# Routing from the un-normalised residual in a two-layer mixture-of-experts stage, with the norm's scale and bias applied after the gather

## The chip, the cores and the metric

The kernel runs on one core of one Trainium2 chip. The metric is device time in microseconds (us) of one execution, as a median over runs. Four blocks run one after the other in it: two layers of attention and mixture of experts (layers 0 and 1), then a recurrent block and a windowed-attention block. The change touches the first two.

## What is computed

From the reference, for each of the two layers (T = 256 tokens, D = 1024, 16 experts of 512 columns, two experts for each token, all fp32):

```python
mix = hybrid_mixer(x, ...)                                    # its last step: concatenate(...) @ w_o
x = layer_norm(ALPHA * x + mix, ln1_g[l], ln1_b[l])
ffn = grouped_moe(x, router_w, router_bias, w_gate[l], w_up[l], w_down[l])
x = layer_norm(ALPHA * x + ffn, ln2_g[l], ln2_b[l])

def grouped_moe(h, router_w, router_bias, w_gate, w_up, w_down):
    aff = sigmoid(xt @ router_w)
    biased = aff + router_bias
    # best group of four experts by its top two, then the top two experts of that group
    wts = aff of the two, divided by their sum
    act = silu(xt @ w_gate[e]) * (xt @ w_up[e]) * gates[e]
    out = sum over e of act @ w_down[e]
```

Only the tokens that chose an expert need its product. The normalised row is (x - mean) * rstd * g + b; mean and rstd belong to the token, g and b to the column.

## The kernel before

Activations stand as two tiles of 128 tokens by 1024 columns (`xn`) and, transposed, as a high and a low fp32r part (`xh`, `xl`). A product with a weight is three fp32r products: high by high, low by high, high by low.

**End of the mixer.** `down` multiplies by `w_o` into four PSUM banks `y[token tile][column half]`. Its last four row chunks run token tile by token tile, so `y[0][0]` is ready about three banks ahead of `y[1][1]`. `layer_norm` then adds the residual, takes the moments (BN_STATS, BN_AGGREGATE, a square root on ScalarE), applies mean, g, rstd and b on VectorE, and transposes the result on TensorE; `logits` multiplies the transposed rows by the split router weights `rwhl`, and `router` turns logits into choices: a sigmoid, then a chain of some thirty small VectorE instructions that ends in the slot numbers `rs` and the one-hot matrices `P`.

**The experts.** `slots(g)` gathers the tokens of four experts as a matrix product of `P` with the rows `xnh`, `xnl` into `xTe`, and turns `P` and the gates (`pgt`, `pgs`, tile `gs`). Eight pairs of experts follow: `gate_up(p)` (`pgg`, then `pgu`), the transpose `pat`, `down` (`pdn`) for the pair before, and `spread`, which adds a pair's output into the four banks `py`. Each of `pgg`, `pgu` and `pdn` is 32 matmuls and uses four chunks of weights.

**The weights.** A layer has 96 chunks of 1 MB (two DMAs of 512 KB each), numbered 0 to 95 in the order of their use: per pair four for `pgg`, four for `pgu`, and four for `pdn` of the pair before. All go through SyncE's queue, which issues in order: a DMA that waits for its buffer holds up all that follow. The first 23 chunks (`FILL`, one letter each) have buffers of their own: `r` the ring, digits places that come free when the mixer's pools close, `m` the tile `misc`, `p` an `xh`/`xl` pair of buffers, `x` the tile `xn` itself. From chunk 23 on only the ring and the numbered places are used again, 18 in all, each as soon as TensorE has read it. `chunks()` asks for the first 23 before the first matmul of the experts.

`py` starts as a matmul that clears the bank and a ScalarE copy of ALPHA times `xn`. After that `xn` is free, so its chunk can load.

In both kernels TensorE's order in the experts is that of the program; on the other engines a scheduler sets the order when the kernel is built, and each engine then works in that order.

## Time and profile before

| | |
|---|---|
| median of 3 runs (1371.28 to 1372.64) | 1371.29 us |
| the profiled execution | 1371.13 us |
| its span, first to last instruction | 1369.5 us |
| TensorE busy | 1306.6 us, 95% |
| VectorE busy | 763.1 us, 56% |
| ScalarE busy | 583.2 us, 43% |
| GpSimd busy | 81.0 us, 6% |
| moved by DMA | 342.93 MB |

The span leaves out about 1.6 us that lie around the instructions. A busy TensorE is not TensorE at its peak, since the ends of matmuls are modelled; the pace of the starts tells more. All places in time below are counted from the start of the span.

### The profile page before, as it was taken

How to read it: one execution, taken by the hardware profiler on the slowest of the kernel's cores; microseconds unless marked ns; L12 is line 12 of the kernel's file. 1: busy time of each engine (PE TensorE's matmuls, PEld its weight loads, DVE VectorE, ACT ScalarE, POOL GpSimd, SP SyncE). 2: the span in 40 equal slices, each digit the busy share in tenths (PEclk: the TensorE clock that was granted, in tenths of full speed). 3: DMA queues.
4: the chain of work that ended last, by engine and by line, in shares of the span. 5: the costliest groups of instructions: out<-in, count | busy, mean ns of one | idle time of the engine just before them, and what ended most of it. 6: DMA issues, size and time to landing. Idle time of an engine off the chain costs nothing.

```text
span 1369.5 us, 20419 instructions
## 1 busy us (share of the span) xinstructions
PE 1306.6 (95%) x7941; PEld 955.6 (70%) x7941; DVE 763.1 (56%) x1584; ACT 583.2 (43%) x1110; POOL 81.0 (6%) x90
## 2 busy tenths in 40 slices
PE   7899899999998998999998999999999999999997
PEld 6787443444487664434435888889998887899986
DVE  4775510111368562111115678879886678888845
ACT  5684410101256841101103524556665376566642
POOL 3000100000200010000002143000000010000000
PEclk9999999999999999999999999999999999999999
DMA  9566699999981767999998820466554365575500
GB/s 299 192 236 256 240 408 398 416 418 416 324 304 70 277 244 290 393 416 417 417 416 290 287 96 29 157 214 214 185 202 136 126 216 171 181 234 185 199 18 31
DMA packets 153448, 342.93 MB, mean 250 GB/s; under 512 B 13282, under 2 KB 84840, under 8 KB 153345
## 3 DMA queue, kind: packets, MB, share of 16 engines
q1 hardware_dynamic: 149408, 330.14, 65.4%
q0 software_dynamic: 3616, 11.15, 2.4%
q8 instruction: 66, 1.08, 0.3%
q10 hardware_dynamic: 320, 0.26, 0.1%
q14 instruction: 38, 0.30, 0.1%
HBM read 340.44 MB, written 1.07 MB: 249 GB/s over the span
## 4 chain that ended last, share of the span: by engine, by line
PE 52%; DVE 3%; ACT 1%; issue 1%; DMA 0%; POOL 0%; DVEq 0%; ACTq 0%
PE pb L174 20%; PE y L174 12%; PE pv L174 3%; PE pdn L174 3%; PE pgg L174 3%; PE pgu L174 3%; PE pl L174 2%; PE ptk L174 2%; DVE xn L362 1%; PE py L174 1%; PE pkv L174 1%; PE po L174 1%; PE pt L228 1%; PE pg L174 1%; DVE wl L168 1%
## 5 line engine op out<-in xcount | busy, mean ns | idle before, releaser
L168 DVE TENSOR_TENSOR wl<-raw,wh 128x1024 fp32r<-128x1024 f32 (+1 forms) x208 | 248.3, 1199 | 86.2 <-ACT wh L167 84.3
L167 ACT ACTIVATE wh<-raw 128x1024 fp32r<-128x1024 f32 (+1 forms) x208 | 213.7, 1035 | 70.2 <-PE y L174 62.1
L1067 DVE SCALAR_TENSOR_TENSOR misc<-misc,gs,pgu 128x512 f32<-128x512 f32 x16 | 12.0, 747 | 226.8 <-PE pgu L174 149.8
L174 PE MATMUL pb<-xh,wh 128*128 128x256 f32 (+1 forms) x944 | 133.6, 281 | 0.5 <-ACT wh L167 0.5
L174 PE MATMUL pb<-xh,wl 128*128 128x256 f32 (+1 forms) x944 | 132.5, 281 | 1.6 <-DVE wl L168 1.6
L174 PE MATMUL pb<-xl,wh 128*128 128x256 f32 (+1 forms) x944 | 132.5, 280 | 0.0
L174 PEld LDWEIGHTS pb<-xh,wh 128*128 128x128 f32 (+1 forms) x944 | 120.3, 187 | 2.1 <-ACT wh L167 0.7
L174 PEld LDWEIGHTS pb<-xh,wl 128*128 128x128 f32 (+1 forms) x944 | 119.9, 187 | 2.2 <-DVE wl L168 2.0
L174 PEld LDWEIGHTS pb<-xl,wh 128*128 128x128 f32 (+1 forms) x944 | 119.9, 187 | 0.1
L174 PE MATMUL pgu<-raw,xTe 128*64 128x512 f32 x512 | 112.6, 592 | 0.0
L174 PE MATMUL pdn<-raw,misc 128*64 128x512 f32 x496 | 109.6, 592 | 0.0
L174 PE MATMUL pgg<-raw,xTe 128*64 128x512 f32 x448 | 103.0, 612 | 4.9 <-PEq L919 4.9
L167 ACT ACTIVATE xh<-pdn 128x512 fp32r<-128x512 f32 x32 | 19.1, 597 | 195.6 <-PE pdn L174 195.6
L174 PEld LDWEIGHTS pgu<-raw,xTe 128*64 128x64 f32 x512 | 37.7, 137 | 72.2 <-issue 68.7
L174 PEld LDWEIGHTS pdn<-raw,misc 128*64 128x64 f32 x496 | 36.4, 137 | 69.4 <-issue 64.4
L174 PEld LDWEIGHTS pgg<-raw,xTe 128*64 128x64 f32 x448 | 32.8, 140 | 65.1 <-issue 58.7
L168 DVE TENSOR_TENSOR xl<-pdn,xh 128x512 fp32r<-128x512 f32 x32 | 21.9, 686 | 100.4 <-ACT xh L167 88.5
L174 PE MATMUL y<-wl,gh 128*128 128x512 f32 x176 | 68.7, 390 | 0.0
L174 PE MATMUL y<-wh,gl 128*128 128x512 f32 x176 | 68.6, 390 | 0.0
L174 PE MATMUL y<-wh,gh 128*128 128x512 f32 x176 | 68.2, 389 | 0.0
L1066 ACT ACTIVATE misc<-pgg 128x512 f32<-128x512 f32 x16 | 9.6, 597 | 128.0 <-PE pgg L174 128.0
L174 PE MATMUL y<-wh,xl 128*128 128x512 f32 x128 | 51.4, 403 | 0.0
(357 smaller groups left out, 2267.1 us busy)
## 6 DMA issues: line engine op xcount, KB each, us to landing
raw<-in_w_up SPq DMA_DIRECT2D x128, 512.0 KB, 9.9
raw<-in_w_down SPq DMA_DIRECT2D x124, 512.0 KB, 9.9
raw<-in_w_gate SPq DMA_DIRECT2D x112, 512.0 KB, 10.0
raw<-in_ffn_w_in SPq DMA_DIRECT2D x44, 1024.0 KB, 6.0
raw<-in_ffn_w_out SPq DMA_DIRECT2D x22, 1024.0 KB, 5.1
raw<-in_hgrn_w_in SPq DMA_DIRECT2D x16, 1024.0 KB, 8.4
raw<-in_w_o SPq DMA_DIRECT2D x8, 1024.0 KB, 11.4
raw<-in_w_in SPq DMA_DIRECT2D x6, 1024.0 KB, 7.9
```

What stands on the lines that cost most here:

```text
L167: nc.scalar.activation(h, src, AF.Copy)
L168: (nc.gpsimd if pool else nc.vector).tensor_tensor(l, src, h.bitcast(F32), op=ALU.subtract)
L174: s.last = s.nc.tensor.matmul(out, lhsT, rhs, start=start, stop=stop, skip_group_check=True).ins
L228: return s.nc.tensor.transpose(out, in_, s.ident[:k, :k])
L362: prev.append(f(*a, **k).ins)
L1066: nc.scalar.activation(sg, ps[0], AF.Silu)
L1067: v.scalar_tensor_tensor(ac, sg, gs[:, p:p + 1], ps[1], op0=ALU.mult, op1=ALU.mult)
```

## The change

**Router.** The layer norm ahead of the experts is gone as a step of its own. TensorE transposes the raw residual r = ALPHA * x + mix. The router weights are multiplied by g and made free of their column mean on the chip (`router_weights`, once per layer, written behind the last weight split of `down`): with W the weights times g less their mean, r @ W times rstd plus a constant `rc` (from b) is the old logit. `aff` is formed by one VectorE instruction per token tile, with rstd as its scalar.

**Rows.** ScalarE writes (r - mean) * rstd, without g and b, into `xn` and `xnh`. `xnl` is made on GpSimd for token tile 0 and on VectorE for token tile 1. The gather's eviction applies g and b, which stand there as one scalar per partition (`gp`).

**First gather.** `slots(0)` uses eight PSUM banks at once, with the products of `xnl` of token tile 1 last, and all eight evictions behind them. Its `pgt`/`pgs` part moves between `pgg` and `pgu` of pair 0. Later calls use four banks at a time.

**Residual.** `py` is now formed by eight VectorE instructions (L1084: x * ALPHA * g in place; L1085: plus ALPHA * b into the bank) in place of four ScalarE copies. g and b as whole rows come by two DMAs on GpSimd's queue into an `xh`/`xl` pair (`gb1`).

**Loads.** The letters `p` and `x` are no longer in the first list; they are asked for behind `residual()`.

The diff, cut to its core:

```diff
-WARM_ROUTER = 8, 4
-WARM_LN = 12
+WARM_ROUTER = 14, 4
...
-    FILL = "rrrmr76rr54rr321rrp0ppx"
+    FILL = "rrrmr76rr54rr321rr0pppx"
...
+    def router_weights(s, li, t):
+
+
+        nc, v = s.nc, s.nc.vector
+        e3 = lambda o: t[:, o:o + 128].rearrange("p (k e) -> p k e", k=8)
+        rw, gw, bw, ones = e3(0), e3(128), e3(256), t[:, 384:512]
+        sums = t[:, 512:544].rearrange("p (a e) -> p a e", a=2)
+
+        with s.tc.issue_after(s.low):
+            v.memset(ones, 1.0)
+            for i, d in enumerate((gw, bw)):
+                v.tensor_tensor(d, rw, s.ln1(li, i)[:, :, None].to_broadcast([128, 8, 16]), op=ALU.mult)
+        p = s.pb("prw")
+        s.mm(p[:, :256], ones, t[:, 128:384], True, True)
+        v.tensor_reduce(sums, p[:, :256].rearrange("p (a k e) -> p a e k", a=2, k=8), axis=AX.X, op=ALU.add)
+        v.tensor_copy(s.rc, sums[:, 1])
+        v.tensor_scalar(sums[:, 0], sums[:, 0], 1.0 / D, None, op0=ALU.mult)
+        v.tensor_tensor(gw, gw, sums[:, 0, None, :].to_broadcast([128, 8, 16]), op=ALU.subtract)
         h = s.rwhl[:, :, 0:16]
-        keep(nc.scalar.activation(h, rw, AF.Copy))
-        keep(nc.vector.tensor_tensor(s.rwhl[:, :, 16:32], rw, h.bitcast(F32), op=ALU.subtract))
+        nc.scalar.activation(h, gw, AF.Copy)
+        v.tensor_tensor(s.rwhl[:, :, 16:32], gw, h.bitcast(F32), op=ALU.subtract)
...
-            gb = s.load_gb(mp, A["ln1_g"][li], A["ln1_b"][li], "kT")
+            rw = s.router_rows(mp.tile([128, 2048], F32, tag="kT", name="rw"))
...
-            s.lg = []
-            s.down(mh, ml, A["w_o"][li], 8, gb,
-                   after0=lambda: s.lg.append(s.logits(0)))
-
-    def down(s, mh, ml, w, nk, gb, col=None, out=None, hold=4, after0=None, pre=None, pool=()):
+            return s.down(mh, ml, A["w_o"][li], 8, None, pre=lambda: s.router_weights(li, rw))
...
+        def moments(b, q):
+            x = s.xn[:, b, q * 512:(q + 1) * 512]
+            seq(v.scalar_tensor_tensor, x, x, ALPHA, y[b][q], op0=ALU.mult, op1=ALU.add)
+            p = s.pb("pt")
+            for j in range(4):
+                s.tr(p[:, j * 128:(j + 1) * 128], x[:, j * 128:(j + 1) * 128])
+            pv = p.rearrange("p (a t) -> p a t", a=4)
+            h, l = (m.t[q][:, :, b * 128:(b + 1) * 128] for m in (xh, xl))
+            seq(act, h, pv, AF.Copy)
+            seq(v.bn_stats, st[b][:, q], x)
+            if q:
+                seq(v.bn_aggr, mv[b][:, 0:2], st[b])
+                seq(act, mv[b][:, 2:3], mv[b][:, 1:2], AF.Sqrt, bias=s.eps[:, 0:1])
+            return lambda: seq(v.tensor_tensor, l, pv, h.bitcast(F32), op=ALU.subtract)
...
+        def affinity(b):
+            lg = s.st.tile([32, 128], F32, tag="lg", name="lg", bufs=2)
+            seq(v.tensor_copy, lg, s.logits(b, xh, xl))
+            p = s.pb("psg")
+            with s.tc.issue_after(last_y):
+                s.mm(p[:, :16], lg, s.two, True, True)
+            return lambda: seq(v.scalar_tensor_tensor, aff[:, b], p[:, :16], mv[b][:, 3:4], s.rc, op0=ALU.mult,
+                               op1=ALU.add)
+
+        def normalized(b):
+            x = s.xn[:, b]
+            seq(act, x, x, AF.Identity, scale=mv[b][:, 3:4], bias=mv[b][:, 4:5])
+            seq(act, xnh[:, b].rearrange("p (c q) -> p c q", c=8), x.rearrange("p (q c) -> p c q", c=8), AF.Copy)
+
+        def low_rows(e, b, c):
+            n, h, l = (t[:, b].rearrange(f, c=8)[:, c] for t, f in ((s.xn, "p (q c) -> p c q"),
+                                                                 (xnh, "p (c q) -> p c q"), (xnl, "p (c q) -> p c q")))
+            return e.tensor_tensor(l, n, h.bitcast(F32), op=ALU.subtract)
...
+        with s.tc.high_priority():
+            low = [moments(0, 0), moments(0, 1)]
+            for f in low:
+                f()
+            scales(0)
+            low = moments(1, 0)
+            normalized(0)
+            seq(v.memset, pick, -BIG_NEG)
+            seq(v.memset, gs[:, 0], BIG_NEG)
+            low()
+            aff0 = affinity(0)
+            s.tc.keep_in_program_order(low_rows(nc.gpsimd, 0, slice(0, 8)))
+            low = moments(1, 1)
+            seq(act, sm[:, 0], s.eps, AF.Sigmoid)
+            gb = [x.rearrange("p a b -> p (a b)").bitcast(F32) for x in s.pair()]
+            for x, a in zip(gb, (s.A["ln1_g"][li], s.A["ln1_b"][li])):
+                s.tc.keep_in_program_order(nc.gpsimd.dma_start(x, bass.AP(tensor=a.tensor, offset=a.offset,
+                                                                          ap=[[0, 128], [1, D]])))
+            aff0()
+            low()
+            scales(1)
+            affinity(1)()
+            seq(act, aff, aff, AF.Sigmoid)
+            normalized(1)
...
-            py = [[s.pa("py") for _ in range(2)] for _ in range(2)]
-            for b in range(2):
-                for dh in range(2):
-
-                    s.mm(py[b][dh], s.negI, s.mgtb[:, None, :].to_broadcast([128, 4, 128]), True, False)
-                    keep(nc.scalar.activation(py[b][dh], s.xn[:, b, dh * 512:(dh + 1) * 512], AF.Copy, scale=ALPHA))
+            low_rows, gb1, ga, ov, rs, cnt = s.router(li, mp, y, xnh, xnl)
+            py = [[], []]
+
+            def residual():
+
+
+                for b in range(2):
+                    for dh in range(2):
+                        py[b].append(s.pa("py"))
+
+                        s.mm(py[b][dh], s.negI, s.mgtb[:, None, :].to_broadcast([128, 4, 128]), True, False)
+                for b in range(2):
+                    for dh in range(2):
+                        c = slice(dh * 512, (dh + 1) * 512)
+                        x = s.xn[:, b, c]
+                        v.scalar_tensor_tensor(x, x, ALPHA, gb1[0][:, c], op0=ALU.mult, op1=ALU.mult)
+                        v.scalar_tensor_tensor(py[b][dh], gb1[1][:, c], ALPHA, x, op0=ALU.mult, op1=ALU.add)
...
-            first = [i for i in range(n0) if i != m]
+            first = [i for i in range(n0) if i != m and s.FILL[i] not in "px"]
...
+                step = 4 if g else 8
+                for c0 in range(0, 8, step):
+
+                    ps = [(s.pa if i > 3 else s.pb)("pg") for i in range(step)]
+
+                    for bs in ((0, xnh), (0, xnl), (1, xnh)), ((1, xnl),):
+                        for c in range(c0, c0 + step):
+                            for b, x in bs:
+                                rhs = P[:, b].rearrange("p e s -> p (e s)")
+                                s.mm(ps[c - c0][:, :T], x[:, b, c * 128:(c + 1) * 128], rhs, b == 0 and x is xnh,
+                                     b == 1 and x is xnl)
+                    for c in range(c0, c0 + step):
+                        p, ga_, be = ps[c - c0][:, :T], s.gp[:, li, 0, c:c + 1], s.gp[:, li, 1, c:c + 1]
+                        if c % 2:
+                            nc.scalar.activation(xt[:, c], p, AF.Identity, scale=ga_, bias=be)
+                        else:
+                            i = v.tensor_scalar(xt[:, c], p, ga_, be, op0=ALU.mult, op1=ALU.add).ins
...
+            def gate_up(p, between=None):
                 x = xTe[p // 2][:, :, (p % 2) * 128:(p % 2) * 128 + 128]
                 ps = []
                 for nm in ("pgg", "pgu"):
+                    if ps and between:
+                        between()
...
+                P, i = onehot(0)
+                with s.tc.issue_after(i):
+                    for c in (0, 4):
+                        low_rows(v, 1, slice(c, c + 4))
+                i = slots(0, P)
                 for p in range(8):
-                    ac = gate_up(p)
+                    ac = gate_up(p, None if p else lambda: gates(0, P))
+                    if not p:
+                        with s.tc.issue_after(i):
+                            residual()
+
+                        for j in range(n0):
+                            load(j)
```

Three places in the built order show what moved. SyncE, layer 0, before: `raw` are the ring and the numbered places, `xh`/`xl` the letters `p`, `misc` the letter `m`, `xn` the letter `x`; the last row is the first chunk of a second use.

```order
L147 DMA raw_1759<-in_w_down 128x1024 x2
L147 DMA xh_1762<-in_w_down 128x1024
L147 DMA xl_1763<-in_w_down 128x1024
L147 DMA misc_1527<-in_w_gate 128x1024 x2
L147 DMA raw_1768<-in_w_down 128x1024 x2
L147 DMA xh_1771<-in_w_gate 128x1024
L147 DMA xl_1772<-in_w_gate 128x1024
L147 DMA xh_1775<-in_w_gate 128x1024
L147 DMA xl_1776<-in_w_gate 128x1024
L147 DMA xn_69<-in_w_gate 128x1024 x2
L147 DMA raw_1959<-in_w_gate 128x1024 x2
```

The same place in the changed kernel:

```order
L146 DMA raw_1743<-in_w_down 128x1024 x2
L146 DMA raw_1746<-in_w_down 128x1024 x2
L146 DMA misc_1450<-in_w_gate 128x1024 x2
L146 DMA xh_1816<-in_w_down 128x1024
L146 DMA xl_1817<-in_w_down 128x1024
L146 DMA xh_1820<-in_w_gate 128x1024
L146 DMA xl_1821<-in_w_gate 128x1024
L146 DMA xh_1824<-in_w_gate 128x1024
L146 DMA xl_1825<-in_w_gate 128x1024
L146 DMA xn_69<-in_w_gate 128x1024 x2
L146 DMA raw_1973<-in_w_gate 128x1024 x2
```

The order is nearly the same; the buffers are others. The third pair (`xh_1824`, `xl_1825`) is now the one that holds g and b for `residual()`, and `xn` is read by `residual()` too. The reuse of the ring stands behind both.

VectorE around pair 0 before, from the first gather's evictions to the copy of `pat`:

```order
L1037 COPY xTe<-pg 128x256 x4
L1050 COPY gs<-pgs 64x2 x2
L1023 TENSOR_TENSOR P<-c,R 128x256 x2
L1067 SCALAR_TENSOR_TENSOR misc<-misc,gs,pgu 128x512
L1074 COPY misc<-pat 128x512
```

And after:

```order
L1142 TENSOR_SCALAR xTe<-pg,gp 128x256 x4
L1084 SCALAR_TENSOR_TENSOR xn<-xn,xh 128x512 x4
L1161 COPY gs<-pgs 64x2 x2
L1119 TENSOR_TENSOR P<-c,R 128x256 x2
L1180 SCALAR_TENSOR_TENSOR misc<-misc,gs,pgu 128x512
L1085 SCALAR_TENSOR_TENSOR py<-xl,xn 128x512 x4
L1187 COPY misc<-pat 128x512
```

The first half of the residual (L1084) stands right behind the gather; the second half (L1085), the last reader of `xn` and of the pair's `xl`, stands behind the instruction that takes `pgu` of pair 0 (L1180).

TensorE at the end of `down` after the change; before, the same matmuls of `y` ran without `plt` between them, and `plt` came after two more transposes of token tile 1:

```order
L228 MATMUL pt<-c,xn 128x128 x4
L174 MATMUL plt<-xh,rwhl 32x128 x8
L174 MATMUL plt<-xl,rwhl 16x128 x8
L174 MATMUL y<-wl,xh 128x512
L174 MATMUL y<-wh,xl 128x512
L174 MATMUL y<-wh,xh 128x512
L174 MATMUL y<-wl,xh 128x512
L174 MATMUL y<-wh,xl 128x512
L174 MATMUL psg<-c,lg 128x16
L228 MATMUL pt<-c,xn 128x128 x4
```

The transposes and logits of token tile 0 now run inside the matmuls of `y`, and delay its last bank by their own time.

## Rows read from the trace of the kernel before

**Rows 1.** The page: what DMA moved in 40 equal slices of the span, GB/s.

```profile
GB/s 299 192 236 256 240 408 398 416 418 416 324 304 70 277 244 290 393 416 417 417 416 290 287 96 29 157 214 214 185 202 136 126 216 171 181 234 185 199 18 31
```

**Rows 2.** Timeline, TensorE, layer 0: start, length, line, operation, count [idle before].

```profile
162.47 5.37 PE L174 MATMUL pgg<-raw,xTe 128*64 128x512 f32 x24
...
169.39 7.04 PE L174 MATMUL pgu<-raw,xTe 128*64 128x512 f32 x32
177.34 0.66 PE L228 MATMUL pat<-c,misc 128*128 128x128 f32 x4 [0.92 <-DVE misc L1067]
...
348.16 7.04 PE L174 MATMUL pdn<-raw,misc 128*64 128x512 f32 x32
...
359.44 7.09 PE L174 MATMUL pdn<-raw,misc 128*64 128x512 f32 x32
```

**Rows 3.** Timeline, SyncE's DMA issues, layer 0.

```profile
150.51 1.36 SPq L147 DMA_DIRECT2D xn<-in_w_gate  x2
164.45 0.80 SPq L147 DMA_DIRECT2D raw<-in_w_gate  x2
...
326.10 18.93 SPq L147 DMA_DIRECT2D raw<-in_w_down  x16
```

**Rows 4.** Windows of layer 0: busy time by engine, granted clock, DMA share, GB/s.

```profile
158.00:160.00 2.00, 2.00 (x14) 2.00 (x14) 0.42 (x1) 0.76 (x2) 0.00 (x0) 0.73 0.05 12
...
170.00:180.00 10.00, 9.09 (x44) 3.06 (x42) 1.44 (x2) 1.52 (x2) 0.00 (x0) 1.00 1.00 375
...
210.00:220.00 10.00, 10.00 (x50) 3.39 (x48) 0.75 (x1) 0.60 (x1) 0.00 (x0) 1.00 0.99 351
...
300.00:310.00 10.00, 10.00 (x65) 6.84 (x62) 3.53 (x7) 2.35 (x5) 0.00 (x0) 1.00 1.02 416
```

**Rows 5.** DMA issues of 335 to 340 us: count, KB each, us to landing.

```profile
raw<-in_w_down SPq DMA_DIRECT2D x5, 512.0 KB, 9.9
```

**Rows 6.** The same of 343 to 346 us.

```profile
raw<-in_w_down SPq DMA_DIRECT2D x2, 512.0 KB, 12.6
...
gb<-in_ln_b POOLq DMA_DIRECT2D x1, 512.0 KB, 8.7
```

**Rows 7.** Timeline, VectorE, from the last residual add to the one-hot matrices.

```profile
138.28 0.69 DVE L362 SCALAR_TENSOR_TENSOR xn<-xn,y 128x512 f32<-128x512 f32 x1
...
140.83 2.20 DVE L362 SCALAR_TENSOR_TENSOR xn<-xn,mv,gb 128x512 f32<-128x512 f32 x3
...
149.47 1.69 DVE L862 TENSOR_TENSOR R<-R,rb 128x32 f32<-128x32 f32 x1 [2.24 <-ACT R L861]
...
155.28 0.40 DVE L1023 TENSOR_TENSOR P<-c,R 128x256 fp32r<-128x256 f32 x1
```

**Rows 8.** Timeline, GpSimd, layer 0.

```profile
145.32 5.78 POOL L981 TENSOR_TENSOR xnl<-xn,xnh 128x1024 fp32r<-128x1024 f32 x2 [55.38 <-PE plt L174]
```

**Rows 9.** Timeline, ScalarE, layer 0.

```profile
137.34 0.60 ACT L332 ACTIVATE xh<-pt 128x512 fp32r<-128x512 f32 x1 [3.11 <-PE pt L228]
```

**Rows 10.** Timeline, TensorE, layer 0, end of `down` to the first gather.

```profile
137.84 0.40 PE L174 MATMUL y<-wh,xl 128*128 128x512 f32 x1
...
141.10 1.03 PE L174 MATMUL py<-mgtb,negI 128*128 128x512 bf16 x4
...
146.04 0.87 PE L174 MATMUL plt<-xl,rwhl 128*16 128x128 f32 x8
...
156.14 0.56 PE L174 MATMUL pg<-P,xnh 128*128 128x256 f32 x1
...
158.84 0.39 PE L174 MATMUL pg<-P,xnh 128*128 128x256 f32 x1
...
161.29 0.27 PE L228 MATMUL pgt<-c,P 128*128 128x128 f32 x1
```

**Rows 11.** Timeline, layer 1: SyncE's first reuse, and TensorE's last `pdn`.

```profile
526.54 0.80 SPq L147 DMA_DIRECT2D raw<-in_w_gate  x2
...
721.31 7.09 PE L174 MATMUL pdn<-raw,misc 128*64 128x512 f32 x32
```

More of the change, by code (lines that the diff above doesn't have):

```diff
@@ L167, in split @@
                 nc.scalar.activation(h, src, AF.Copy)
-                (nc.gpsimd if pool else nc.vector).tensor_tensor(l, src, h.bitcast(F32), op=ALU.subtract)
+                i = (nc.gpsimd if pool else nc.vector).tensor_tensor(l, src, h.bitcast(F32), op=ALU.subtract)
+                s.low = i.ins
             else:
@@ L272, in more_consts @@
         nc.gpsimd.dma_start(rows[26:27], A["hgrn_gnorm_w_2"])
-        rv = A["router_w"].rearrange("(k p) e -> p k e", p=128)
+        nc.gpsimd.dma_start(rows[27:43], A["ln1_g"].rearrange("l (k p) -> (l k) p", p=128))
+        nc.gpsimd.dma_start(rows[43:59], A["ln1_b"].rearrange("l (k p) -> (l k) p", p=128))
+        s.gp = s.cp.tile([128, 2, 2, 8], F32, name="gp")
+        for i, n in enumerate(("ln1_g", "ln1_b")):
+            nc.gpsimd.dma_start(s.gp[:, :, i], A[n].rearrange("l (p k) -> p l k", k=8))
@@ L274, in more_consts, with router_rows, columns @@
+        return rows
+    def router_rows(s, t):
+        rv = s.A["router_w"].rearrange("(k p) e -> p k e", p=128)
         for k in (0, 4):
-            nc.gpsimd.dma_start(rw[:, k:k + 4], rv[:, k:k + 4])
-        return rows, rw
-    def columns(s, rows, rw):
-        nc = s.nc
+            s.nc.gpsimd.dma_start(t[:, 16 * k:16 * k + 64].rearrange("p (k e) -> p k e", k=4), rv[:, k:k + 4])
+        return t
+    def columns(s, rows):
         p = s.pb()
         keep = s.tc.keep_in_program_order
-        keep(s.tr(p[:, :27], rows[:27]))
-        keep(nc.vector.tensor_copy(s.col[:, :27], p[:, :27]))
-        s.rwhl = s.cp.tile([128, 8, 32], F32R, name="rwhl")
+        keep(s.tr(p[:, :59], rows[:59]))
+        keep(s.nc.vector.tensor_copy(s.col[:, :59], p[:, :59]))
@@ L346, in load_gb, with layer_norm @@
         return gb
-    def layer_norm(s, y, gb, out=None, added=False, after0=None):
+    def layer_norm(s, y, gb, out=None, added=False):
         nc, v = s.nc, s.nc.vector
@@ L607, in mixer @@
             if li == 0:
-                s.columns(*rows)
+                s.columns(rows)
             def index_scores(b):
@@ L770, in mixer, with down @@
             s.attn_out(pp3, lambda j, sb: dv[:, sb], mh, ml, 6, mp)
-            s.lg = []
-            s.down(mh, ml, A["w_o"][li], 8, gb,
-                   after0=lambda: s.lg.append(s.logits(0)))
-    def down(s, mh, ml, w, nk, gb, col=None, out=None, hold=4, after0=None, pre=None, pool=()):
+            return s.down(mh, ml, A["w_o"][li], 8, None, pre=lambda: s.router_weights(li, rw))
+    def down(s, mh, ml, w, nk, gb, col=None, out=None, hold=4, pre=None, pool=()):
         y = [[s.pa("y") for _ in range(2)] for _ in range(2)]
@@ L799, in down @@
                             mul(k, tb, q, H, L)
-        if out is None:
+        if out is None and gb is not None:
             s.xh, s.xl = s.new_xT()
@@ L807, in down @@
                     mul(k, tb, q, H, L)
-        s.layer_norm(y, gb, out, after0=after0)
+        if gb is None:
+            return y
+        s.layer_norm(y, gb, out)
     def tr_hl(s, n, nch, h, l):
@@ L825, in proj_w, with logits @@
             evac(cb, p[:, :T])
-    def logits(s, b):
+    def logits(s, b, xh, xl):
         p = s.pb("plt")[:32, :128]
@@ L833, in logits, with router @@
         for k in range(8):
-            s.mm(p, s.rwhl[:, k], s.xh.k(k, t), k == 0, False)
+            s.mm(p, s.rwhl[:, k], xh.k(k, t), k == 0, False)
         for k in range(8):
-            s.mm(p[:16], s.rwhl[:, k, 0:16], s.xl.k(k, t), False, k == 7)
-        lg = s.st.tile([32, 128], F32, tag="lg", name="lg", bufs=2)
-        s.nc.vector.tensor_copy(lg, p)
-        return lg
-    def router(s, mp):
+            s.mm(p[:16], s.rwhl[:, k, 0:16], xl.k(k, t), False, k == 7)
+        return p
+    def router(s, li, mp, y, xnh, xnl):
         nc = s.nc
@@ L853, in router @@
         sm = mp.tile([128, 3, 2], F32, name="sm")
-        v.memset(pick, -BIG_NEG)
-        v.memset(gs[:, 0], BIG_NEG)
-        s.tc.keep_in_program_order(nc.scalar.activation(sm[:, 0], s.eps, AF.Sigmoid))
-        s.lg.append(s.logits(1))
-        p = s.pb("psg")
-        for b in range(2):
-            s.mm(p[:, b * 16:(b + 1) * 16], s.lg[b], s.two, True, True)
-        nc.scalar.activation(R[:, 0], p[:, :32], AF.Sigmoid)
+        st = [s.st.tile([128, 2, 6], F32, tag="bst", name="bst", bufs=2) for _ in range(2)]
@@ new lines, in router, with seq @@
+        mv = [s.st.tile([128, 8], F32, tag="mv", name="mv", bufs=2) for _ in range(2)]
+        xh, xl = s.new_xT()
+        last = {}
+        def seq(f, *a, **k):
+            e = f.__self__
+            with ExitStack() as es:
+                if id(e) in last:
+                    es.enter_context(s.tc.issue_after(last[id(e)]))
+                last[id(e)] = f(*a, **k).ins
+        act = nc.scalar.activation
+        last_y = s.last
+        def moments(b, q):
[12 more added lines that the diff above has]
+            return lambda: seq(v.tensor_tensor, l, pv, h.bitcast(F32), op=ALU.subtract)
```

72 lines of the change are left out of this document (28 added, 44 removed).

## Prediction

> **What bounds the kernel now.** I read the page's slices first. DMA moves 390 to 418 GB/s in two stretches [rows 1]: these are the two expert stages, and everything that the change touches lies at their start. The question for each is what sets its end.
>
> TensorE's timeline answers it. In layer 0 the experts start at 162.47 us. A group of 32 matmuls takes about 7.04 us from first to last [rows 2], that is 7.0/4 = 1.75 us for each chunk of weights. The groups at 169.39 and at 348.16 take the same: TensorE runs at one pace at both ends of the stage, so weights do not hold it up. The last `pdn` ends at 359.44 + 7.09 = 366.5.
>
> Beside it stands the stream of weights, which is slower. In full flow it moves 416 GB/s [rows 4], 1.05 MB / 416 = 2.52 us a chunk. So TensorE gains on it through the whole stage, and lives on what was loaded ahead. Before, all 23 first chunks are issued by 150.51 + 1.36 = 151.9, the queue then has nothing to do (12 GB/s in 158 to 160 [rows 4]), and the first reuse goes out at 164.45 [rows 3], 2.0 us after the experts start, when their first chunk has been read.
>
> How much lead is left at the end? The last 16 DMAs are issued in 326.10 to 345.03 [rows 3], about 1.25 us apart. The eighth, the end of chunk 91, leaves at about 334.9 and lands 9.9 us later [rows 5], at 344.8. TensorE reaches that chunk at 348.16 + 3 x 1.75 = 353.4: lead 8.6 us. Chunk 95 leaves at 344.7 and lands 12.6 later [rows 6], at 357.3; it is needed at 359.44 + 5.25 = 364.7: lead 7.4 us. That is the number on which the forecast turns: **if the stream falls back against TensorE by more than some 8 us, it becomes the bound of the stage.**
>
> **The change, part by part (layer 0).**
>
> *End of `down`.* `prw`, two more sets of four transposes and `plt` of token tile 0 now run ahead of the last matmul of `y`. `plt` is two sets of eight; eight take 0.87 us from first start to last end, and some 0.4 of that is the last one's own end [rows 10], so a set holds TensorE for 0.47. `prw` is not in the trace; an fp32 product of 256 columns costs between 0.28 (a row of a gather at full clock) and twice 0.56 (at half clock) [rows 10]; I take 0.4. With 0.95 for `plt`, 0.7 for the transposes (eight, between 0.06 each, as `plt`, and 0.12, as a gather's step; I take the middle) and 0.45 for a square root that the residual add of tile 1 now waits for, the last bank is done 2.5 us later: 137.84 + 0.40 + 2.5 = 140.7.
>
> *From there to `P`.* Residual add 0.69 [rows 7], transpose 0.6, ScalarE's high part 0.60 [rows 9] (behind the normalised rows of tile 0, about 0.65 us late), low part 0.69, then logits, copy, `psg`, affine, sigmoid and bias: 2.0 us, an estimate of some 0.3 us each. The bias add ends at 145.9. Before it ended at 149.47 + 1.69 = 151.16 [rows 7]. The thirty small instructions behind it do not change: 155.68 - 151.16 = 4.5 us, so `P` is done at 150.4.
>
> The 1.69 us stood out: an add of 128x32 took that long while GpSimd made `xnl` until 145.32 + 5.78 = 151.10 [rows 8]. With one half of `xnl` on GpSimd, begun at about 142.7, the add is free of it; if it, or the small scale instructions of tile 1, still meet it, 0 to 1.7 us are added. I take 0, since 142.7 + 2.9 = 145.6. [...]
>
> *First gather.* Before, its first 12 steps ran at (158.84 - 156.14)/12 = 0.225 us and the rest at (161.29 - 158.84)/20 = 0.12 [rows 10]; the clock was 0.73 of full in 158 to 160 [rows 4]. TensorE now waits under 1 us ahead of it, so I take 0.12 throughout: 3.8 us from 150.9 (half a microsecond behind `P`, as before), less the eight last matmuls over which the evictions can start, plus one eviction of about 0.45. **The experts start at 154.3, 8.2 us earlier.** At half clock throughout it would be 156; nothing lets it start before 152.5, since the router chain and the 24 matmuls that need no late row are a chain.
>
> `pgt`/`pgs` (162.47 - 161.29 = 1.2 us) and the clearing of `py` (1.03 [rows 10]) come back inside pair 0. From pair 1 on TensorE is 6 us ahead of before. With four banks the three later gathers cost between 0 and 0.5 us each; I take 0.4: 4.8 us are left at the end, if nothing else holds.
>
> *The loads.* Here is the price. Chunk 21's second buffer and chunk 22's (`xn`) come free after L1085. VectorE reaches L1085 behind the instruction that takes `pgu`, so only after all of pair 0: 154.3 + 6.92 + 1.2 + 7.03 (169.39 to 176.42, where `pgu` was taken [rows 2]) + 0.75 for that instruction + 4 x 0.73 (three of these took 2.20 [rows 7]) = 173.1. SyncE is in order, so the whole reuse of the ring waits behind it. TensorE and VectorE do not feel this; the stream does. It resumes 173.1 - 164.45 = 8.7 us later than before, with one and a half chunks more to bring: 3.8 us. It gets some back: before, it ran at 375 and at 351 GB/s in two windows where the ring was full [rows 4], worth 10 x (41 + 65)/416 = 2.6 us. **Net: the stream is 9.9 us later than before, in absolute time.**
>
> The lead of 7.4 us does not cover that. Chunk 95 lands at 367.2, and the last group ends 1.75 us later, at 368.95: **+2.4 us**. Chunk 91 lands at 354.7; the vectors of the second norm (1.05 MB, 2.5 us of stream) are asked for when a numbered place is read, and now fall ahead of it; then it lands at 357.2, and with the 13.1 us from there to the end (366.5 - 353.4) the stage ends at 370.3: **+3.8 us**. I take the middle, 3.1.
>
> *Layer 1* has the same rows at the same distances: reuse at 526.54, last group ending at 721.31 + 7.09 = 728.4 [rows 11]: 201.9 us apart, against 202.1. Again 3.1 us. The next blocks' first weights follow the stream; they lie behind the norm, and I count nothing for them (bounds 0 and 2 us a layer).
>
> *The rest at nothing.* Router weights are prepared under the matmuls of `y`. The row vectors g and b land by about 154 and are wanted at 154.5; if late by a few microseconds, they delay L1084, still ahead of `pgu`'s end.
>
> **Sum.** 1371.13 + 2 x 3.1 = 1377.3 us. The profiled execution lies 0.16 us under the median, which is no difference.
>
> **The rivals.**
>
> *The stream keeps up* (faster). If the lead is larger than landings show, or the stream resumes sooner, TensorE's gain stays: 2 x 4.8 = 9.6, giving 1361.5. For it: the groups shown keep 7.04 us, and the landing times are medians of a few. Against it: the whole gain stays only if the stream is no more than 7.4 - 4.8 = 2.6 us late, so if it resumes by 165.8. The point from which it decides is a stream 7.4 us late, resumed at 170.6, so an experts' start at 151.8, which is earlier than the chain allows. [...]
>
> *Gain and delay cancel* (within 0.2%, 2.7 us, about what a measurement of this kernel can tell from no change). Start at 153, landings 1 us better: 0 to +1.3 us a layer, 1372.5.
>
> *More is lost* (slower still). The lock with GpSimd (1.7), a gather at half clock (1.7), and the next block's weights (up to 2) each push the same chain: 2 x (3.1 + 3.5) = 13, 1384.
>
> **How the numbers follow.** Forecast 0.5, rival of the kept stream 0.2, cancel 0.2, more lost 0.1. The forecast's own range is 1374 to 1381. For 8 in 10 the range reaches into the cancelled and part of the faster case: 1367 to 1383. Slower by over 0.2%: 0.6; within: 0.2; faster: 0.2.
>
> **What would show it.** The first `pgg` at 153 to 156; SyncE's `xn` load at 172 to 175 and DMA near idle for 15 us before; TensorE waiting for DMA in the last two or three `pdn`/`pgg` groups, which stretch beyond 7.1 us to about 10; the last `pdn` ending at 368 to 371. It is wrong if the groups keep 7.04 us to the end, or if `xn` loads before 169.

## The result, and the profile after

| | before | changed |
|---|---|---|
| device time, median of four runs | 1371.88 us (1371.28 to 1372.64) | 1386.38 us (1383.39 to 1390.76) |
| ratio | | 1.0108, 95% interval 1.0079 to 1.0137 |
| span of the profiled execution | 1369.5 us | 1389.0 us |
| TensorE busy | 1306.6 us | 1322.5 us |

The changed kernel is slower, as forecast, but by 14.5 us and not by 6: the median lies 9 us over the forecast and above its range. The profiled execution is the slowest of the four.

Two lines of the page of the changed kernel: what DMA moved in 40 slices [rows 1], and the shares of the chain that ended last, which is the chain of work followed back from the last instruction.

```profile
GB/s 293 190 216 264 145 375 408 409 409 408 366 322 116 244 203 177 410 408 409 409 409 385 313 109 44 122 186 246 193 193 116 160 215 137 187 254 182 185 29 30
...
PE 61%; DMA 28%; DVE 7%; ACT 2%; issue 1%; SPq 1%; POOL 0%; DVEq 0%; ACTq 0%
```

The same line of the kernel before:

```profile
PE 52%; DVE 3%; ACT 1%; issue 1%; DMA 0%; POOL 0%; DVEq 0%; ACTq 0%
```

The two lines don't cover the same time: before, the chain could be followed back only to 592 us, in layer 1, and from there to the end of that stage it is TensorE's. In the changed kernel it reaches to the start, and in layer 0 it runs from the resume of the loads to chunk 91 as one DMA behind the other (start, length, what):

```profile
176.83 7.92 DMA raw<-in_w_gate
...
184.77 10.21 DMA raw<-in_w_up
...
349.96 12.77 DMA raw<-in_w_down
...
362.78 1.93 PE pdn L174 x6
```

So the stream has become the bound of the stage. In full flow it moves 409 GB/s where it moved 416 to 418. That was in no step of the forecast.

TensorE in layer 0 of the changed kernel, as [rows 2]: start, length, count, and in brackets the idle time before a group and what ended it.

```profile
156.38 5.37 PE L174 MATMUL pgg<-raw,xTe 128*64 128x512 f32 x24
...
171.65 1.04 PE L174 MATMUL py<-mgtb,negI 128*128 128x512 bf16 x4
...
322.95 7.47 PE L174 MATMUL pdn<-raw,misc 128*64 128x512 f32 x32
332.80 7.85 PE L174 MATMUL pgg<-raw,xTe 128*64 128x512 f32 x32
...
347.42 2.35 PE L174 MATMUL pgu<-raw,xTe 128*64 128x512 f32 x8 [1.22 <-DMA raw<-in_w_up]
...
354.78 2.67 PE L174 MATMUL pdn<-raw,misc 128*64 128x512 f32 x8 [1.43 <-DMA raw<-in_w_down]
...
362.78 1.93 PE L174 MATMUL pdn<-raw,misc 128*64 128x512 f32 x6 [0.21 <-DMA raw<-in_w_down]
368.96 7.09 PE L174 MATMUL pdn<-raw,misc 128*64 128x512 f32 x32
```

The experts start 6.1 us earlier than before and end 9.5 us later, at 376.05 instead of 366.53. Groups that took 7.04 us stretch from 323 us on, then break into pieces, the wait ahead of each ended by a DMA. The very last group is whole again: the piece at 362.78 (chunk 91) is the last that waits.

SyncE's issues in the same stretch [rows 3].

```profile
160.01 0.33 SPq L146 DMA_DIRECT2D xh<-in_w_gate  x1
175.02 0.33 SPq L146 DMA_DIRECT2D xl<-in_w_gate  x1
175.44 0.86 SPq L146 DMA_DIRECT2D xn<-in_w_gate  x2
176.40 1.23 SPq L146 DMA_DIRECT2D raw<-in_w_gate  x2
...
340.03 23.05 SPq L146 DMA_DIRECT2D raw<-in_w_down  x16
```

And VectorE: the bias add, the instruction that takes `pgu`, and the residual that SyncE waits for.

```profile
147.83 0.19 DVE L954 TENSOR_TENSOR R<-R,rb 128x32 f32<-128x32 f32 x1 [0.29 <-ACT R L888]
...
171.83 0.75 DVE L1180 SCALAR_TENSOR_TENSOR misc<-misc,gs,pgu 128x512 f32<-128x512 f32 x1 [5.98 <-issue]
172.50 2.50 DVE L1085 SCALAR_TENSOR_TENSOR py<-xl,xn 128x512 f32<-128x512 f32 x4
```

L1085 ends at 175.00 and `xl` is asked for at 175.02. The first reuse of the ring goes out at 176.40 instead of 164.45; the 16 last issues of `w_down` end at 363.08 instead of 345.03: 18 us later, against a lead of 8.6.

Windows of the changed kernel [rows 4]: the first lies in the stretch in which the queue is nearly empty, the second reaches past its resume at 175; the others are full flow in both layers.

```profile
160.00:170.00 10.00, 10.00 (x56) 4.01 (x54) 1.07 (x4) 1.20 (x2) 0.00 (x0) 1.00 0.16 52
170.00:180.00 10.00, 10.00 (x49) 3.37 (x46) 3.76 (x6) 0.00 (x0) 0.00 (x0) 1.00 0.39 140
190.00:340.00 150.00, 145.21 (x727) 64.61 (x724) 23.97 (x45) 17.98 (x32) 0.00 (x0) 1.00 1.03 409
560.00:710.00 150.00, 145.35 (x726) 64.42 (x722) 23.98 (x45) 17.97 (x32) 0.00 (x0) 1.00 1.03 409
```

Layer 1 takes 371.9 us from the end of layer 0's experts (376.05) to its own last `pdn` (747.91), where it took 361.9 (366.53 to 728.4 [rows 2, 11]). 9.5 and 10.0 us are the whole difference of the spans, 19.5.

### The profile page after: what moved, and what is told of

The parts are those of the page before. It is cut to its first block, busy times and chain, and to the rows that moved or that the text cites. A ratio compares the mean times of both kernels' runs of the same rounds, so it can differ in the third digit from the quotient of the medians.

```text
span 1389.0 us, 20438 instructions
## 1 busy us (share of the span) xinstructions
PE 1322.5 (95%) x7933; PEld 957.9 (69%) x7933; DVE 769.8 (55%) x1611; ACT 587.6 (42%) x1107; POOL 79.1 (6%) x94
## 4 chain that ended last, share of the span: by engine, by line
PE 61%; DMA 28%; DVE 7%; ACT 2%; issue 1%; SPq 1%; POOL 0%; DVEq 0%; ACTq 0%
PE pb L174 23%; PE y L174 15%; DMA raw<-in_w_down 9%; DMA raw<-in_w_up 9%; DMA raw<-in_w_gate 8%; PE pv L174 3%; PE sc L174 3%; PE po L174 2%; PE pl L174 2%; PE ptk L174 2%; PE ptp L228 1%; PE pk L174 1%; PE pdn L174 1%; PE pgu L174 1%; PE pgg L174 1%
## 5 line engine op out<-in xcount | busy, mean ns | idle before, releaser
L1180 DVE SCALAR_TENSOR_TENSOR misc<-misc,gs,pgu 128x512 f32<-128x512 f32 x16 | 12.0, 748 | 215.8 <-PE pgu L174 152.5
L174 PE MATMUL pdn<-raw,misc 128*64 128x512 f32 x496 | 117.6, 595 | 6.7 <-DMA raw<-in_w_down 6.7
L174 PE MATMUL pgu<-raw,xTe 128*64 128x512 f32 x512 | 118.7, 595 | 2.5 <-DMA raw<-in_w_up 2.3
L174 PE MATMUL y<-wl,xh 128*128 128x512 f32 x128 | 51.6, 404 | 0.0
## 6 DMA issues: line engine op xcount, KB each, us to landing
raw<-in_w_o SPq DMA_DIRECT2D x8, 1024.0 KB, 11.2
```

The costliest lines, as they stand in the source:

```text
L174: s.last = s.nc.tensor.matmul(out, lhsT, rhs, start=start, stop=stop, skip_group_check=True).ins
L1180: v.scalar_tensor_tensor(ac, sg, gs[:, p:p + 1], ps[1], op0=ALU.mult, op1=ALU.mult)
```

## The experiments

Theory: the stream resumes late, behind the residual, and loses more there than TensorE gained. Rivals: the lower rate alone does it; or TensorE's early start is lost in another place. All times are medians, ratios are to the kernel before on the same chip. The pads are tiles that nothing uses. In the window of the fourth column the kernel before moves 412 GB/s, and less in its first part, where SyncE waits for room in the ring; its full flow is compared below.

| run | us | ratio, 95% interval | GB/s, 190 to 340 us | `pdn` of layer 0 ends |
|---|---|---|---|---|
| changed, without third pair and `x` | 1363.60 | 0.9937 (0.9920 to 0.9953) | 409 | 363.40 |
| changed, residual first | 1368.96 | 0.9978 (0.9969 to 0.9988) | 409 | 369.96 |
| before, residual late | 1390.01 | 1.0132 (1.0115 to 1.0149) | 416 | 375.18 |
| changed, again | 1387.93 | 1.0110 (1.0093 to 1.0127) | 409 | 373.78 |
| changed, 192 bytes of pad | 1381.21 | 1.0070 (1.0052 to 1.0088) | 416 | 371.79 |
| before, 320 bytes of pad | 1372.09 | 1.0003 (0.9993 to 1.0012) | 407 | 366.13 |
| first, 192 bytes of pad | 1363.82 | 0.9942 (0.9924 to 0.9960) | 416 | 364.28 |
| first, places aligned | 1362.81 | 0.9935 (0.9918 to 0.9953) | 419 | 363.65 |
| aligned, four banks | 1363.14 | 0.9935 (0.9918 to 0.9951) | 419 | 363.00 |
| aligned, low row on GpSimd | 1370.47 | 0.9994 (0.9984 to 1.0003) | 419 | 365.70 |
| ring 96 bytes off | 1363.16, one run | | 417 | |
| numbered places 64 off | 1358.08, one run | | 417 | |

### Is it the late stream?

**No weights behind the residual.**

```diff
-    FILL = "rrrmr76rr54rr321rr0pppx"
+    FILL = "rrrmr76rr54rr321rr0pp"
```

> The changed kernel without the third pair and the residual's tile among the places of the first 23 chunks (21 remain), so that no weight load stands behind the residual on SyncE's queue. Theory (the stream resumes late, behind the residual's last read at 176 us, and loses there what TensorE gained): the ring's first reuse is issued at 163 to 165 us in layer 0 instead of 176.4; the two chunks that no longer go there cost 3.8 us in the ring, so the last w_down issue comes 9 us earlier (354) at the 409 GB/s of the changed kernel's profile, 12 to 13 us earlier (350) at the 417 of the kernel before; time 1365 (at 417) to 1373 us (at 409). Rival (the loss sits in the rate alone, or in the mixer's 2.3 us): the resume hardly matters and the time stays at 1383 to 1391 us.

SyncE's first reuse and TensorE's last two `pdn` groups in that run:

```profile
156.35 4.37 SPq L146 DMA_DIRECT2D raw<-in_w_gate  x6
```

```profile
345.02 7.04 PE L174 MATMUL pdn<-raw,misc 128*64 128x512 f32 x32
...
356.31 7.09 PE L174 MATMUL pdn<-raw,misc 128*64 128x512 f32 x32
```

The reuse goes out 2.0 us after the experts' start (154.38), as in the kernel before, which is 7 us sooner than I had expected. No group waits, at 409 GB/s, and the time lies under the 1373 us that I had expected for that rate. The whole loss is gone and the kernel is 8.8 us faster than before. One line of the change decides its sign; the rival of the rate alone falls.

**The residual ahead of pair 0.**

```diff
+                with s.tc.issue_after(i):
+                    residual()
                 for p in range(8):
                     ac = gate_up(p, None if p else lambda: gates(0, P))
                     if not p:
-                        with s.tc.issue_after(i):
-                            residual()
```

> The changed kernel with the residual's four TensorE steps and eight VectorE instructions ahead of the first gate product instead of behind pair 0; all places kept. Theory: the third pair and the residual's tile come free at 161 to 162 us, the stream resumes there instead of at 175 to 176, the last w_down issue comes 13 us earlier than in the changed kernel (350), TensorE is the bound again by 1 to 4 us: 1363 to 1368 us. The first gate product starts 4 us later (160.5), which costs nothing since the same four steps are gone from behind pair 0. Rival (place of the residual is no matter, the rate is): 1383 to 1391 us. Rival (TensorE's early start is lost anyway): 1372 us.

The resume came at 161.6 to 164.2 and the stage ended without a wait for weights, as the theory says. The time is 1 us over the upper end of the forecast. In the profiled execution, its slowest (span 1374.0), a group of pair 2 took 10.09 us instead of 7.09, at a granted clock of 0.50 in 230 to 235 us, and the experts started at 158.7, with 0.86 us in which `py` waited for an eviction.

```profile
157.72 1.05 PE L174 MATMUL py<-mgtb,negI 128*128 128x512 bf16 x4 [0.86 <-ACT xTe L1140]
...
174.96 0.66 PE L228 MATMUL pat<-c,misc 128*128 128x128 f32 x4 [0.92 <-DVE misc L1180]
```

That the later start costs nothing did not hold. Against the first run the gather begins 2.4 us later here (152.69 against 150.27), and pair 1 4.3 later (175.54 against 171.22): 1.9 us come from the residual's new place, since TensorE now waits ahead of `pat` for nearly as long as the four steps took there. If layer 1 is alike, that is 3.8 of the 5.4 us between the two medians; the rest is not settled.

**The late residual alone, in the kernel before.** The four `py` steps and ScalarE's copies go behind pair 0:

```diff
-            first = [i for i in range(n0) if i != m]
+            first = [i for i in range(n0) if i != m and s.FILL[i] != "x"]
...
                     ac = gate_up(p)
+                    if not p:
+                        residual()
+                        for j in range(n0):
+                            load(j)
```

> The kernel before with one thing of the change alone: the residual's four TensorE steps and ScalarE copies behind pair 0, and the load into the residual's tile behind them; the router, the norm and the gathers stay as they were. Theory: the ring's first reuse is issued at about 181 us instead of 164.45 (pair 0 ends at 176.5, then four steps of 1.03 us), one more chunk of 2.5 us is left to load; against a lead of 8.6 us the end of the stage is 10 to 11 us later in each layer: 1392 us at 417 GB/s, 1399 at 409. Rival (the stream catches up, the loss of the changed kernel is elsewhere): only the four TensorE steps on the path, 4 us in each layer at most, 1372 to 1380 us.

```profile
177.15 1.36 SPq L147 DMA_DIRECT2D xn<-in_w_gate  x2
178.61 0.86 SPq L147 DMA_DIRECT2D raw<-in_w_gate  x2
```

1390.0 us, 2 under the forecast, with the reuse at 178.61 instead of 181: this one part makes the old kernel as slow as the changed one, with the old router and the higher rate. With the first run it shows the cause from both sides.

### Where does 409 GB/s come from?

**The changed kernel again**, to see whether rate and time vary together.

> The changed kernel as it is. Theory (it is bound by the stream, and its runs differ by the stream's rate): where the profile shows 417 GB/s in 190 to 340 us, the last w_down issue of layer 0 comes at about 359.5 and the time is 1383 to 1384; at 409 GB/s 363 and 1391. Rival (the rate of 409 belongs to this program): 409 again whatever the time, and the runs' spread has another cause. TensorE's half clock at 69 to 72 us of the mixer (1.6 us): with it the first half of the mixer ends 2.3 us later than in the kernel before, without it 0.7.

```profile
153.94 5.37 PE L174 MATMUL pgg<-raw,xTe 128*64 128x512 f32 x24
```

```profile
172.58 0.33 SPq L146 DMA_DIRECT2D xl<-in_w_gate  x1
173.00 0.86 SPq L146 DMA_DIRECT2D xn<-in_w_gate  x2
173.95 0.93 SPq L146 DMA_DIRECT2D raw<-in_w_gate  x2
```

409 again, at 1388 us and not 1391: my theory that the rate varies between executions fell. All profiles of the changed program so far had 409, those of the old one 416 to 418 in full flow. This execution has no half clock in the mixer (1.00 granted in 66 to 76 us), and starts the experts 2.4 us earlier than the first profile.

What else differs between the programs? The new tiles in the pool of constants had moved every weight place in SBUF up by 320 bytes.

**Pads.** 192 more bytes put the changed kernel's places back where the old ones lie, modulo 512; 320 bytes move those of the kernel before to where the change has them.

```diff
         s.col = s.cp.tile([128, 60], F32, name="col")
+        s.cp.tile([128, 48], F32, name="pad")
```

```diff
         s.col = s.cp.tile([128, 32], F32, name="col")
+        s.cp.tile([128, 80], F32, name="pad")
```

> The changed kernel with an unused tile of 192 bytes for each partition in the pool of constants, and no other edit: every weight place then lies as far from a multiple of 512 bytes as in the kernel before (the change had moved all of them up by 320 bytes). So far the stream ran at 409 GB/s in all four profiles of the changed kernel and its variants, and at 416 to 417 in the two of the kernel before and its variant. Theory (the rate comes from where the places lie): 416 to 417 GB/s in 190 to 340 us, the last w_down issue of layer 0 3.4 us earlier from the same resume, the stage 3.4 us shorter in each layer: 1380 to 1382 us. Rival (the rate comes from something else in the program): 409 GB/s and 1386 to 1389 us.

> The kernel before with an unused tile of 320 bytes for each partition in the pool of constants: all weight places lie where the changed kernel has them. Theory (rate by place): 409 GB/s, the last w_down issue of layer 0 at about 348.5 instead of 345.0, the stream's lead of 8.6 us down to 5, and the time unchanged, 1371 to 1373 us, since TensorE is still the later one. Rival: 416 to 417 GB/s. Both give the same time; the rate tells them apart.

The full-flow window of the changed kernel with the pad:

```profile
190.00:340.00 150.00, 145.20 (x732) 64.52 (x728) 23.97 (x45) 18.54 (x33) 0.00 (x0) 1.00 1.03 416
```

The kernel before waits for room in the ring at the start of that window, so its full flow is read behind 230 us; without the pad, then with it:

```profile
230.00:330.00 100.00, 99.78 (x500) 44.31 (x502) 13.71 (x27) 10.25 (x20) 0.00 (x0) 0.98 1.03 416
```

```profile
230.00:330.00 100.00, 100.00 (x502) 44.20 (x501) 13.72 (x27) 10.24 (x20) 0.00 (x0) 0.98 1.03 409
```

The rate goes with the places, both ways. It is worth 5 to 6 us to the changed kernel (14.5 and 15.6 over before without the pad, in two measurements, 9.6 with it) and nothing to the kernel before, whose lead covers it: there the last issue ends at 346.99, 2.0 us later than without the pad (3.5 were expected), and TensorE is still the later one.

**The same pads without the third pair.** The second run has 416 bytes and, in the stage's pool, 32, so that all places lie at multiples of 512. Both have the shorter `FILL` of the first run; the aligned one further:

```diff
         s.col = s.cp.tile([128, 60], F32, name="col")
+        s.cp.tile([128, 104], F32, name="pad")
...
             gs = mp.tile([128, 8], F32, name="gs")
+            mp.tile([128, 8], F32, name="pad")
```

> The changed kernel without the third pair and the residual's tile among the first places, and with the 192 bytes. TensorE sets the end of the stage already without them (no wait for a weight load stood at the end of its stage), so a faster stream should give little: 1362 to 1364 us, with 417 GB/s by the theory of the places and 409 by its rival.

> As the run without the third pair and the residual's tile, with 416 bytes in the pool of constants and 32 in the stage's pool, so that every weight place begins at a multiple of 512 bytes. Theory of the places: the rate changes with the place, at least 417 GB/s here (the kernel before, with the higher rate, has eight of its 18 ring places at a multiple of 256 and ten at 32 past one); if the multiple is what counts, over 417. Rival: 409. Time 1362 to 1364 us either way, since TensorE is the later one.

```profile
190.00:340.00 150.00, 145.77 (x728) 64.68 (x726) 24.06 (x45) 18.67 (x33) 0.98 (x2) 0.99 1.03 419
```

416 and 419, and no difference in time, as expected: TensorE is the later one. The aligned one lies 0.65% under before (0.47 to 0.82%); its interval overlaps those of the two beside it, so none of the three is shown to be the fastest.

**One half of the places off at a time**: the ten places of the rotating ring 96 bytes past a multiple of 256, or the eight numbered ones 64 past. The pads of the aligned version become, in turn:

```diff
-        s.cp.tile([128, 104], F32, name="pad")
+        s.cp.tile([128, 128], F32, name="pad")
...
-            mp.tile([128, 8], F32, name="pad")
+            mp.tile([128, 48], F32, name="pad")
```

```diff
-            mp.tile([128, 8], F32, name="pad")
+            mp.tile([128, 24], F32, name="pad")
```

> The run with the places aligned, but the ten places of the rotating ring moved to 96 bytes past a multiple of 256; the eight numbered places stay at a multiple. Rates so far by (ring, numbered places), bytes past a multiple of 256: (32, 0) 416, (96, 64) 409, (0, 0) 419. Theory A (what counts is only whether a place is off a multiple of 256): the ring's ten of 18 places are off as in the kernel before, so 416 to 417 GB/s. Theory B (how far off it is counts): 96 costs more than 32, and the rate is 412 to 414. No difference in time is expected (1362 to 1364 us), since TensorE is the later one.

> The other half: the ring at a multiple of 256, the eight numbered places 64 bytes past one. Theory A: eight of 18 places off, 417 GB/s. Theory B, with the two halves adding up to what the changed kernel lost: 413 to 415 GB/s. Time 1362 to 1364 us.

Each half alone costs 2 GB/s, both together 10. My theory of how far off (412 to 415) fell for both. That the loss is small while some places are aligned, and large when none is, is what was measured; why is open. The 1358.08 is a single run; it supports no verdict. Both groups behind the overflow check took 7.09 us in it, at a granted clock of 1.00 (220 to 240 and 580 to 600 us), but that alone does not explain it: in the profile of the four-bank run below neither ran at half clock (1.00 granted in 190 to 340 and in 560 to 710), at 1365.40.

### Two parts of TensorE's gain

**Four banks** for the first gather, in the aligned version.

```diff
-                step = 4 if g else 8
+                step = 4
```

> The run with the places aligned (1362.8 us, bound by TensorE), with one part of the change undone: the first gather in four PSUM banks, two times four columns, instead of eight banks at once. Theory: eight banks let TensorE run 24 steps before it needs the late row, and the evictions come once; with four, the second half waits for the first half's evictions, whose VectorE part stands behind the low row of tile 1: the first gate product starts 0.7 to 1.5 us later (155.5 to 156.3 instead of 154.8), 1364 to 1366 us. Rival (the banks give nothing): 154.8 and 1363.

```profile
153.38 0.39 PE L174 MATMUL pg<-P,xnh 128*128 128x256 f32 x1 [0.42 <-ACT xTe L1142]
...
155.86 5.37 PE L174 MATMUL pgg<-raw,xTe 128*64 128x512 f32 x24 [0.29 <-DVE xTe L1144]
```

The second half waits for an eviction and the experts start 1.0 us later (155.86 against 154.83), as expected; the time, 0.3 us more where 1 to 3 were expected, does not resolve it.

**The low row of tile 1 on GpSimd**, in the aligned version.

```diff
-                with s.tc.issue_after(i):
-                    for c in (0, 4):
-                        low_rows(v, 1, slice(c, c + 4))
+                s.tc.keep_in_program_order(low_rows(nc.gpsimd, 1, slice(0, 8)))
```

> The run with the places aligned, with the low row of token tile 1 as one GpSimd instruction instead of two on VectorE. GpSimd needs 2.9 us for it and would run at 149.5 to 152.4, beside the router's last small instructions and the one-hot matrices. Theory (VectorE instructions with two SBUF operands and GpSimd's hold one another up; the bias add of 128x32 that took 1.69 us in the kernel before): one of these VectorE instructions takes over 2 us, the one-hot matrices end near 153.3 instead of 151.0, the first gate product starts 2 to 3 us later (157 to 158), 1367 to 1369 us. Rival (no such hold): the one-hot matrices end at 151.0, and the start is 154.8 or a little earlier, 1362 to 1363.

GpSimd's row and VectorE's, from that run:

```profile
149.19 2.84 POOL L930 TENSOR_TENSOR xnl<-xn,xnh 128x1024 fp32r<-128x1024 f32 x1 [2.23 <-ACT xnh L889]
```

```profile
149.30 2.77 DVE L987 TENSOR_SCALAR R<-R 128x32 f32<-128x32 f32 x1
```

An instruction of 0.18 us is held for 2.77 until GpSimd is done (149.19 + 2.84 = 152.03; 149.30 + 2.77 = 152.07). The one-hot matrices end 2.2 us later and the experts start at 158.46, 3.6 later, where 2 to 3 were expected: TensorE has by then idled 2.6 us, and the first half of the gather runs at 0.21 us a step instead of 0.12, the pace that the kernel before had at a granted clock of 0.50 in 156 to 158. 7.7 us in all by the medians, 1.5 over the range; in the two profiles it is 2.0 at the end of layer 0, where the aligned run has a group of 8.78 us (granted clock 0.91 in 220 to 240) and this one has no such dip (1.00 in 190 to 340), and 4.1 in layer 1. The hold is real, and the changed kernel escapes it by its placement. This instruction has a single tensor input; the bias add that took 1.69 us before [rows 7], and 0.19 here ahead of GpSimd's row, has two. The recurrent block of the kernel before shows both kinds held: a TENSOR_TENSOR of 128x256 took 0.42 us at 826.82, and 0.84 at 836.21, where it ended 0.28 behind GpSimd's instruction; a TENSOR_SCALAR of 128x256 took 0.30 at 823.91, and 0.74 at 829.31 beside GpSimd. Not all are: in the changed kernel a TENSOR_SCALAR of 128x1 took 0.21 at 146.15, during GpSimd's `xnl`. What decides it is not shown.

## Why the prediction was right in direction and short in size

Layer 0; "again" and "pad" are the profiles of the changed kernel run again, and with 192 bytes of pad.

1. *The lead of 7 to 9 us decides.* Right. With the last issues 18 us later the stage ends 9.5 us later; in the late-residual run 17 and 8.7.
2. *The experts start at 154.3.* Right: 153.94 (again), 154.50 (pad), though partly by luck: in the first of these the gather begins at 149.87, a microsecond ahead of the 150.9 in the sum, and then takes 4.1 us to the first product and not 3.4. The first profile's 156.38 is an execution whose mixer ran partly at half clock (0.50 in 70 to 72 us). The bias add met no GpSimd (0.19 us), and the gather ran at 0.12 a step.
3. *The stream resumes at 173.1 behind L1085.* Right: `xl` at 172.58 and 173.14, with about 13 us of near idleness before it (28 GB/s in 160 to 173.14 with the pad), and SyncE in order behind it: `raw` at 173.95 in the first.
4. *It gets 2.6 us back, and is 9.9 us later.* Right up to the fifth of the last 16 issues, off by 1.3 from there on. With the pad, at the old rate, the fifth leaves at 340.80, 9.75 us later than before (331.05). The next leaves 2.75 us behind it, where 1.2 to 1.3 are usual, and so chunk 91 leaves at 346.10, 11.2 us later than 334.9. The vectors of the second norm are asked for in that gap, at 341.77; that they cause it is not shown. SyncE before, then SyncE and GpSimd's queue with the pad:

```profile
331.05 0.33 SPq L147 DMA_DIRECT2D raw<-in_w_down  x1
```

```profile
340.80 0.33 SPq L146 DMA_DIRECT2D raw<-in_w_down  x1
...
343.55 0.33 SPq L146 DMA_DIRECT2D raw<-in_w_down  x1
```

```profile
341.77 0.53 POOL L377 DMA_DIRECT2D gb<-in_ln_g  x1 [194.81 <-DMA raw<-in_w_up]
```

5. *The middle of chunk 91's and chunk 95's result, 3.1 us.* This step failed in its reasoning, and measured 5.3 us: the end of a stage is set by the later of two chunks, not by their mean. The chain of waits of the run with the pad (start, length, what) shows which:

```profile
346.10 12.40 DMA raw<-in_w_down
...
358.54 1.93 PE pdn L174 x6
```

Chunk 91 lands at 358.50 (forecast 357.2), 12.4 us after it left instead of 9.9 [rows 5]; an extra of 2.5, as much as the forecast had for the norm's vectors on this chunk; that they cause it is not shown. From there to the end it is 13.3 us, forecast 13.1. So: 3.1 forecast, + 0.7 for the later chunk, + 1.3 for the stream, + 0.2 = 5.3 us, as measured (371.79 - 366.53). Layer 1 of that profile, for which the forecast has the same 3.1, loses 6.4.
6. *The stream moves 416 GB/s.* The step that failed most. The forecast took the rate from rows of the kernel before and did not ask whether the change touches it. The stream moved 409: the change's new tiles shift the places. Over some 186 us of stream that is an estimate of 186 x 7/416 = 3.1 us a layer; the pad gives back 5 to 6 us in the two.
7. *Sum.* Forecast +6.2. With places as before +9.6; with the places that the change gives +14.5 to 15.6. So by the medians steps 4 and 5 are 3.4 and step 6 is 4.9 of the 8.3 us that were missing (14.5 - 6.2); the profile with the pad lies 1.6 over its median. Against the changed kernel run again step 6 is 5.9 us.

The rivals: the kept stream, 1361.5 and 4.8 us a layer from TensorE, comes near once the stream is freed: 1363.6, with 3.1 us gained in layer 0 and 4.5 in layer 1 of that profile. But part of this is the clock. The group behind the overflow check took 8.78 and 8.79 us in the kernel before (granted clock 0.91 in 220 to 240 and in 580 to 600), 8.42 and 7.09 here (0.91 and 1.00); without that difference 2.8 us are left in each layer. The term that was too large is the later gathers. From the first `pg` to `pgg` the three of layer 0 took 5.32, 4.91 and 4.91 us before and 6.73, 6.04 and 6.05 here, where TensorE waits twice for an eviction: 1.1 to 1.4 us each, and not 0.4. The second of them, before and in the first run:

```profile
255.04 0.28 PE L174 MATMUL pg<-P,xnh 128*128 128x256 f32 x1
...
259.95 7.09 PE L174 MATMUL pgg<-raw,xTe 128*64 128x512 f32 x32
```

```profile
249.62 0.28 PE L174 MATMUL pg<-P,xnh 128*128 128x256 f32 x1
...
251.94 0.39 PE L174 MATMUL pg<-P,xnh 128*128 128x256 f32 x1 [0.29 <-DVE xTe L1142]
...
255.66 7.09 PE L174 MATMUL pgg<-raw,xTe 128*64 128x512 f32 x32
```

Cancel and more lost: none of the three mishaps of the latter occurred (the lock, put at 1.7 us from the bias add of [rows 7], the slow gather, the next block); the time went there for another reason.

## What to carry to other kernels

Where a slow stream is hidden by a lead, ask of every edit when the stream can resume: a buffer lent to the load queue for one chunk held up all behind it until its last reader was done, since the queue issues in order: the first reuse went out at 176.40 us and not at 164.45. Take a chunk's lead as the least over all chunks, and a stage's end as the latest, never a mean. A tile added to a pool moves the tiles behind it, here by 320 bytes and from 416 to 409 GB/s, so compare the rate of the same transfers before and after.

## What the runs showed of the hardware that was not expected

**The rate of a DMA went with where its destination begins in SBUF.** The same 512 KB transfers of 4 KB pieces ran at 419 GB/s in full flow with all 18 places at multiples of 512 bytes, at 416 to 417 with a part of them off a multiple of 256, and at 409 with all off (by 96 and 64 bytes). A pad moves every tile behind it, and no run moved a destination alone. Why the halves cost 2 GB/s each and both 10 is not shown.

**Half clock comes and goes in the same place.** In the first profile of the changed kernel TensorE's granted clock was 0.50 in 70 to 72 us, behind a gap of 1.06 us in its work, and two matmuls took 0.84 us instead of 0.51:

```profile
70.35 0.84 PE L174 MATMUL pb<-wl,qah 128*128 128x384 f32 x2
```

The kernel before has the same gap, 1.05 us, and kept full clock (1.00 in 70 to 72), and so did the changed kernel when run again (1.00 in 66 to 76). Behind the overflow check, where TensorE waits 2.3 to 2.8 us, the next group took between 7.09 and 10.09 us in different executions. In the three profiles of the old program and its variants it took 8.78 or 8.79 all six times, in the eleven of the changed one over 7.09 in 8 of 22. Such dips are worth 1.3 to 3 us each. They may make up part of the spread of 7 us between the four runs, but only one of the four has a profile.
